# A diffusion layer on one core: a third block normed between value blocks, and the mixer's transfers tied in source order

## The chip, the core and the metric

The kernel runs on one NeuronCore of a Trainium2 chip. The metric is the device time of one execution in microseconds (us). PE is the matrix engine, PEld its weight load, DVE the vector engine, ACT the scalar engine, POOL the GpSimd engine, and SP the engine whose only work here is to issue every DMA of the program, one after the other in the order of its own instruction list.

## What is computed

One layer with fp32 inputs over 17 chunks of 128 tokens: one chunk of context and 16 of latent tokens. The layer norms and modulates its input, projects it, runs a short convolution and a bidirectional gated scan (mLSTM), projects back, and ends with a gated feed-forward network.

```
h = rmsnorm(x, norm1) * (1 + scale1) + shift1
z = h @ w_in                            # sc_b, sc_c, sc_x, q, k, v, o, gates
y_sc = sc_b * conv3(sc_c * sc_x)
h_m = mlstm_bidir(q, k, v, gates)       # per chunk of 128, 4 heads, forward and backward
h_m = rmsnorm(h_m) * mh_norm * sigmoid(o)
x = x + gate1 * (concat(y_sc, h_m) @ w_out)
h2 = rmsnorm(x, norm2) * (1 + scale2) + shift2
up = conv3(h2 @ w_up);  a, gg = split(up)
x = x + gate2 * ((silu(gg) * a) @ w_down);  y = rmsnorm(x, final_norm)
```

## The kernel before

Every large product is made of three: each fp32 operand is split into a rounded high part and a rest (`wh`/`wl` for weights, `hH`/`hL` for activations), and `wh*hH + wh*hL + wl*hH` is added up in a PSUM bank. So a weight tile goes through four steps before PE can use it: a DMA into `wst` (two buffers), a rounding on ACT (`wh`, L111), two subtractions on DVE (`wl`, L114), and then PE. `wh` and `wl` have four buffers each.

The 2176 tokens are six blocks of 384 (the last of 256). Blocks 3 to 5 (`BB`) go first, blocks 0 to 2 (`BA`) second. For `BB`, the value and gate products (`vg`, L378), the k and q heads, the short convolution and the o heads are done in the opening stage, while DVE prepares the modulation beside them. While the o heads of `BB` run, `make_h` norms the blocks of `BA` one by one: `apply` multiplies by the spread inverse norms (DVE, L177), adds the shift on ACT (L181, L185, L186) and takes the rest on DVE (L182, L187), for eight tiles of a block. Then `vg(BA)` follows: per chunk and half one PSUM bank, 24 matmuls, and a small DVE addition (`gates`, L395) that lets go of the bank.

After that come the two woven stages. `weave` walks over units, each a chunk and a pair of heads, 34 in all, and puts blocks of projection work (`fill`) between the units:

- `Sums`: per unit a transposition of k (PE, L792, to PSUM tile `S`), a copy `kT` (ACT, L794), the weighting of v (DVE), two products into `y` (PE, L803), copies of the result (ACT, L814) and a store of the state to `sD`. The fill is the q heads and then the o heads of `BA`: for each head one weight tile, three gemms of 24 matmuls (one for each block), and for each gemm a copy `row` on ACT (L403) and a store to `qD` or `oD` (L404).
- `Mix`: per unit the scores (PE, L850), mask, exponentials and weights (DVE L851, ACT L855, DVE L858 and L859), the output products (PE, L873 and L875), normalization on DVE (L879 to L888), a transposition (PE, L902), the gating by `o` (DVE, L904), and a store to `yD`. It loads k, q, v, the rows `R`, the states `sb` and, in `second`, `o2`. The fill is the short convolution of `BA` (four rounds of three weight tiles and nine gemms, each round ending in stores to `yD`) and then the output projection (`out_proj`, L451): two blocks at a time are loaded back from `yD` (`xt`, two buffers), split on ACT (L461) and DVE (L462), and multiplied by eight weight tiles.

In source order a unit's loads come two units ahead, a head's weights right before its first gemm, and a round's three weights right before its first gemm:

```
            for h in range(H):
                w = load_w(I["w_in"][w0 + h])
                for b in blocks:
                    head(w, b, h, hs, dst, func, scale)
                    yield
```

The source order isn't the program's order. A scheduler takes the traced instructions and orders them engine by engine, under their true dependences; whatever is free of a dependence can be put earlier. SP's list is made in the same way, and an instruction on it that waits for data holds up all the transfers behind it.

Of the kernel before, what the change touches and what calls it, by code (L numbers as in the profile page):

```python
# [2 lines left out]

# [35 lines left out]
BA = (0, 1, 2)  # L39
# [7 lines left out]
def chunks(b):  # L47
    t0, n = BL[b]
    return range(t0 // P, (t0 + n) // P)


def spans(t0, t1):

    return [(a, b, v) for a, b, v in ((t0, min(t1, P), 0), (max(t0, P), t1, 1)) if a < b]
# [3 lines left out]
def hymba_kernel(ctx: ExitStack, tc: tile.TileContext, I, O):  # L58
    nc = tc.nc
# [42 lines left out]
    def run(g, side=None, every=1):  # L102
        for i, _ in enumerate(g):
            if side and i % every == 0:
                next(side, None)

    def load_w(src, n=1024):
        st = wp.tile([P, WN], F32, name="wst", bufs=2)
        Q.dma_start(st[:, :n], src)
        wh = wp.tile([P, WN], F32R, name="wh")  # L110
        S.activation(wh[:, :n], st[:, :n], AF.Copy)  # L111
        wl = wp.tile([P, WN], F32R, name="wl")
        for a in (0, n // 2):
            V.tensor_sub(wl[:, a:a + n // 2], st[:, a:a + n // 2], wh[:, a:a + n // 2].bitcast(F32))  # L114
        return wh, wl
# [18 lines left out]
    def spread(r, n):  # L134

        ps = pst.tile([P, 512], F32, name="st")
        for i in range((n + P - 1) // P):
            w = min(P, n - i * P)
            PE.matmul(ps[:, i * P:i * P + w], bc(r[:w, i:i + 1], [w, P]), ident[:w, :w], start=True, stop=True)
        return ps  # L140

    def load_x(b, src, pool, name, bufs):
        t0, n = BL[b]
        xt = []
        for kh in range(2):
            x = pool.tile([P, 4, 384], F32, name=name, bufs=bufs)
            Q.dma_start(x[:, :, :n], src[4 * kh:4 * kh + 4, :, t0:t0 + n].rearrange("k p t -> p k t"))
            xt.append(x)
        return xt

    def rcol(b):
        t0, n = BL[b]
        return rc[:, t0 // P:(t0 + n) // P]
# [12 lines left out]
        return ss  # L166

    def apply(b, xt, norm):
        t0, n = BL[b]
        rb = spread(rcol(b), n)  # L170
        hH, hL = h_pair()
        sh = 0 if norm == 0 else 24
        for k in range(KT):
            x = xt[k // 4][:, k % 4]
            for a, e, v in spans(t0, t0 + n):
                a, e = a - t0, e - t0
                V.scalar_tensor_tensor(x[:, a:e], x[:, a:e], ab[:, norm, k, v:v + 1], rb[:, a:e],  # L177
                                       op0=ALU.mult, op1=ALU.mult)
                sv = modT[:, sh + k, v:v + 1]
                if k % 2 == 0:  # L180
                    S.activation(hH[:, k, a:e], x[:, a:e], AF.Identity, bias=sv)  # L181
                    V.scalar_tensor_tensor(hL[:, k, a:e], x[:, a:e], sv, hH[:, k, a:e].bitcast(F32),  # L182
                                           op0=ALU.add, op1=ALU.subtract)
                else:
                    S.activation(x[:, a:e], x[:, a:e], AF.Identity, bias=sv)  # L185
                    S.activation(hH[:, k, a:e], x[:, a:e], AF.Copy)  # L186
                    V.tensor_sub(hL[:, k, a:e], x[:, a:e], hH[:, k, a:e].bitcast(F32))  # L187
        return hH, hL

    def h_pair():  # L190
        pool = hps[next(turn) % 3]
        return [pool.tile([P, KT, 384], F32R, name=n) for n in ("hH", "hL")]

    def make_h(b, src, norm):
        return apply(b, load_x(b, src, xp, "xt", 2), norm)

    def accumulator():
        pool = pa[next(turn_a) % len(pa)]
        return pool.tile([P, 512], F32, name="acc")
# [154 lines left out]
    with ExitStack() as ph1:  # L354
        wp = ph1.enter_context(tc.tile_pool(name="wp", bufs=4))
        xp = ph1.enter_context(tc.tile_pool(name="xp", bufs=2))
# [18 lines left out]
        def load_vg(j):  # L375
            return [load_w(I["w_vg"][j, kk], WN) for kk in range(2)]

        def vg(blocks, hs, ws):  # L378
            for b in blocks:
                hH, hL = hs[b]  # L380
                for j in range(2):
                    for c in chunks(b):
                        o = c * P - BL[b][0]
                        acc = accumulator()
                        for k in range(KT):
                            w_h, w_l = (x[:, (k % 4) * 264:(k % 4 + 1) * 264] for x in ws[2 * j + k // 4])
                            a_h, a_l = hH[:, k, o:o + P], hL[:, k, o:o + P]
                            PE.matmul(acc[:, :264], a_h, w_h, start=(k == 0), stop=False)
                            PE.matmul(acc[:, :264], a_h, w_l, start=False, stop=False)
                            PE.matmul(acc[:, :264], a_l, w_h, start=False, stop=(k == KT - 1))  # L390
                        r = rq.tile([P, 2, 129], F32, name="rv", bufs=4)
                        G.memset(r[:, :, 128:129], 1.0)
                        S.activation(r[:, :, :P], acc[:, :256].rearrange("p (h d) -> p h d", h=2), AF.Copy)
                        Q.dma_start(vD[c][:, 2 * j:2 * j + 2], r)
                        V.tensor_add(gates[:, c, j * 8:(j + 1) * 8], acc[:, 256:264],  # L395
                                     bgate[:, j * 8:(j + 1) * 8])
                        yield
# [8 lines left out]
        def heads(blocks, hs, w0, dst, func, scale, by_block=False):  # L406
            if by_block:
                ws = [load_w(I["w_in"][w0 + h]) for h in range(H)]
                for b in blocks:
                    for h in range(H):  # L410
                        head(ws[h], b, h, hs, dst, func, scale)
                        yield
                return
# [5 lines that stand above are left out]
# [89 lines left out]
        hs = {}  # L508
        with tc.tile_pool(name="start", bufs=1, side="right") as stp, \
# [28 lines left out]
            inv_rms(ss, 384, rcol(3))  # L538
            mods(4, 8)
            hs[3] = apply(3, xs[3], 0)  # L540
            ws += load_vg(1)
            Q.dma_start(bgate, I["b_gate"].to_broadcast([P, 16]))
# [24 lines left out]
            def prep(b):  # L567
                xs[b] = load_x(b, I["x"], stp, "xs", 4)
                ss = squares(b, xs[b])
                yield  # L570
                inv_rms(ss, BL[b][1], rcol(b))
                yield
                hs[b] = apply(b, xs[b], 0)
                yield
# [48 lines left out]
            go = heads(BB, hs, 20, oD, AF.Sigmoid, 1.0, by_block=True)  # L623
            for b in BA:
                run(islice(go, 4), side)
                hs[b] = make_h(b, I["x"], 0)
            run(side)
            pa.pop()

# [196 lines left out]
        class Mix:  # L826
# [71 lines left out]
            def third(self):  # L898
# [7 lines left out]
                t0 = (c + 1) * P  # L906
                Q.dma_start(yD[4 + 2 * hp:6 + 2 * hp, :, t0:t0 + P].rearrange("h d t -> d h t"), o2)

        def weave(units, fill, blocks):

            n = len(units)
            for i in range(-1, n + 3):
                if 0 <= i < n:
                    units[i].first()
                if 0 <= i - 3 < n:
                    units[i - 3].third()
                if 0 <= i - 1 < n:
                    units[i - 1].second()
                for x in (0, 1) if i < 0 else (i + 2,):
                    if x < n:  # L920
                        units[x].load()
                for _ in range(blocks[i % 3]):
                    next(fill, None)


        run(vg(BA, hs, load_vg(0) + load_vg(1)))
        with tc.tile_pool(name="gt", bufs=1, side="right") as gt:
            gph = gate_phase()
            kh = heads(BA, hs, 16, kD, AF.Copy, 1.0)
# [11 lines left out]
        for hp in range(2):  # L941
# [6 lines left out]
        fill = chain(heads(BA, hs, 12, qD, AF.Copy, QS), heads(BA, hs, 20, oD, AF.Sigmoid, 1.0),  # L948
                     shortconv(BA, hs), out_proj(((0, 1), (2, 3))))
        weave([Sums(c, hp) for c in range(NL - 1, -2, -1) for hp in range(2)], fill, (1, 0, 1))  # L950
        weave([Mix(c, hp) for c in range(-1, NL) for hp in range(2)], fill, (2, 1, 2))
        phr.close()
        slots = {6: slot(6, "right")}
# [8 lines left out]
        last = out_proj(((4, 5),), late)  # L962
# [10 lines left out]
    with ph2:  # L973
# [219 lines left out]
        for w, (hf, x) in enumerate(PRODS):  # L1193
            n = HN[hf] // 2 // NP[hf]
# [114 lines left out]
```

## Time and profile before

| what | value |
|---|---|
| median of 3 runs | 2507.28 us (2504.99 to 2508.83) |
| profiled execution, its own time | 2504.05 us |
| its span, first to last instruction | 2502.2 us |
| mean granted TensorE clock over the span | 0.992 of full speed |
| PE / PEld / DVE / ACT / POOL busy | 98% / 96% / 69% / 44% / 3% |
| q and o heads with `Sums` (about 500 to 640 us) | PE busy 139.76 of 140 us |
| `Mix` with convolution and output projection (640 to 935 us) | PE busy 285.35 of 295 us |

How to read it: busy times are per engine and overlap. PE's busy share says that it had a matmul in hand, not at which clock; the granted clock stands in the windows view beside it. Times are from the span's start, and L numbers are lines of the kernel before; in the changed kernel the same statements stand some lines further down (L109 and L114 where they were, L404 at L408, L770 at L778, L803 at L811).

### The profile page before, as it was taken

How to read it: one execution, taken by the hardware profiler on the slowest of the kernel's cores; microseconds unless marked ns; L12 is line 12 of the kernel's file. 1: busy time of each engine (PE TensorE's matmuls, PEld its weight loads, DVE VectorE, ACT ScalarE, POOL GpSimd, SP SyncE). 2: the span in 40 equal slices, each digit the busy share in tenths (PEclk: the TensorE clock that was granted, in tenths of full speed). 3: DMA queues.
4: the chain of work that ended last, by engine and by line, in shares of the span. 5: the costliest groups of instructions: out<-in, count | busy, mean ns of one | idle time of the engine just before them, and what ended most of it. 6: DMA issues, size and time to landing. Idle time of an engine off the chain costs nothing.

```text
span 2502.2 us, 44204 instructions
## 1 busy us (share of the span) xinstructions
PE 2454.3 (98%) x17043; PEld 2398.2 (96%) x17043; DVE 1731.5 (69%) x3327; ACT 1100.3 (44%) x2109; POOL 62.9 (3%) x128
## 2 busy tenths in 40 slices
PE   8999999999999989999999999999999999999998
PEld 7999999999999989999999999999999988889998
DVE  4895443433467777789888888776767788677665
ACT  4511133333334444455455445554545454443343
POOL 0000000000011111000000000000000000000000
PEclk9999999999999999999999999999999999999999
DMA  8798723466567886877456446644454476576544
GB/s 276 264 288 257 251 93 112 136 204 205 183 198 213 250 276 198 279 253 259 149 196 217 144 161 212 219 147 168 146 168 147 164 269 233 191 272 207 183 154 151
DMA packets 252437, 506.18 MB, mean 202 GB/s; under 512 B 22962, under 2 KB 153154, under 8 KB 241346
## 3 DMA queue, kind: packets, MB, share of 16 engines
q1 hardware_dynamic: 252226, 503.35, 60.9%
q8 instruction: 134, 2.20, 0.4%
q14 instruction: 77, 0.63, 0.1%
HBM read 355.24 MB, written 148.03 MB: 201 GB/s over the span
## 4 chain that ended last, share of the span: by engine, by line
PE 79%; DMA 8%; DVE 8%; issue 1%; ACT 1%; SPq 1%; POOL 0%; DVEq 0%; ACTq 0%; POOLq 0%
PE pa L1148 7%; PE pa L1150 7%; PE pa L1149 7%; PE acc L206 6%; PE acc L208 6%; PE acc L207 6%; PE pb L1150 4%; PE pb L1148 3%; PE pb L1149 3%; DVE jk L560 3%; PE pa L1206 3%; PE pa L1207 3%; PE pa L1208 3%; DMA wD<-wm 2%; PE pc L1208 2%; PE pc L1206 2%
## 5 line engine op out<-in xcount | busy, mean ns | idle before, releaser
L206 PE MATMUL acc<-hH,wh 128*128 128x384 f32 (+1 forms) x1536 | 514.9, 335 | 5.5 <-DVE cr L430 4.1
L208 PE MATMUL acc<-hH,wl 128*128 128x384 f32 (+1 forms) x1536 | 505.9, 329 | 0.5 <-DVE wl L114 0.5
L207 PE MATMUL acc<-hL,wh 128*128 128x384 f32 (+1 forms) x1536 | 504.9, 329 | 0.0
L1148 PE MATMUL pa<-tH,wh 128*128 128x272 f32 x1408 | 408.5, 290 | 3.8 <-DVE row L488 2.7
L1150 PE MATMUL pa<-tH,wl 128*128 128x272 f32 x1408 | 407.2, 289 | 0.0
L1149 PE MATMUL pa<-tL,wh 128*128 128x272 f32 x1408 | 405.1, 288 | 0.0
L278 ACT ACTIVATE wh<-st 128x512 fp32r<-128x512 f32 (+1 forms) x312 | 189.0, 609 | 403.1 <-PE pa L1149 108.7
L206 PEld LDWEIGHTS acc<-hH,wh 128*128 128x128 f32 x1536 | 291.1, 190 | 8.0 <-DVE cr L430 4.7
L208 PEld LDWEIGHTS acc<-hH,wl 128*128 128x128 f32 x1536 | 290.9, 189 | 1.2 <-DVE wl L114 0.9
L207 PEld LDWEIGHTS acc<-hL,wh 128*128 128x128 f32 x1536 | 291.1, 190 | 0.7
L989 DVE SCALAR_TENSOR_TENSOR tt<-raw,fw,tt 128x127 f32<-128x127 f32 (+4 forms) x264 | 242.3, 947 | 49.3 <-ACT tt L995 48.2
L1148 PEld LDWEIGHTS pa<-tH,wh 128*128 128x128 f32 x1408 | 264.9, 188 | 4.8 <-DVE row L488 2.9
L279 DVE TENSOR_TENSOR wl<-st,wh 128x512 fp32r<-128x512 f32 (+1 forms) x312 | 205.4, 660 | 91.3 <-ACT wh L278 87.9
L1149 PEld LDWEIGHTS pa<-tL,wh 128*128 128x128 f32 x1408 | 265.4, 188 | 0.0
L1150 PEld LDWEIGHTS pa<-tH,wl 128*128 128x128 f32 x1408 | 264.7, 188 | 0.0
L1148 PE MATMUL pb<-tH,wh 128*128 128x272 f32 x704 | 203.6, 289 | 0.4 <-ACT wh L278 0.4
L1150 PE MATMUL pb<-tH,wl 128*128 128x272 f32 x704 | 203.6, 289 | 0.0
L1149 PE MATMUL pb<-tL,wh 128*128 128x272 f32 x704 | 202.7, 288 | 0.0
L278 ACT ACTIVATE wh<-s 128x512 fp32r<-128x512 f32 x176 | 110.9, 630 | 146.5 <-PE pc L1149 90.1
L114 DVE TENSOR_TENSOR wl<-wst,wh 128x512 fp32r<-128x512 f32 (+1 forms) x160 | 105.9, 687 | 64.2 <-ACT wh L111 64.2
L279 DVE TENSOR_TENSOR wl<-s,wh 128x512 fp32r<-128x512 f32 x176 | 120.7, 687 | 29.0 <-ACT wh L278 25.4
L1148 PEld LDWEIGHTS pb<-tH,wh 128*128 128x128 f32 x704 | 132.4, 188 | 0.6 <-ACT wh L278 0.6
(236 smaller groups left out, 5222.0 us busy)
## 6 DMA issues: line engine op xcount, KB each, us to landing
st<-in_w_up SPq DMA_DIRECT2D x88, 512.0 KB, 4.6
wst<-in_w_in SPq DMA_DIRECT2D x48, 512.0 KB, 4.1
wU<-s SPq DMA_DIRECT2D x22, 1024.0 KB, 6.5
s<-wU SPq DMA_DIRECT2D x22, 1024.0 KB, 5.7
st<-wD SPq DMA_DIRECT2D x32, 704.0 KB, 5.2
st<-in_w_down SPq DMA_DIRECT2D x28, 704.0 KB, 4.0
R<-nD SPq DMA_DIRECT2D x34, 512.0 KB, 5.4
wm<-in_w_modr SPq DMA_DIRECT2D x32, 512.0 KB, 3.7
```

The source lines that it names most:

```text
L114: V.tensor_sub(wl[:, a:a + n // 2], st[:, a:a + n // 2], wh[:, a:a + n // 2].bitcast(F32))
L206: PE.matmul(acc[:, :n], w_h, hH[:, k, :n], start=(k == 0), stop=False)
L207: PE.matmul(acc[:, :n], w_h, hL[:, k, :n], start=False, stop=False)
L208: PE.matmul(acc[:, :n], w_l, hH[:, k, :n], start=False, stop=(k == KT - 1))
L278: S.activation(wh[:, :n], a, AF.Copy)
L279: V.tensor_sub(wl[:, :n], a, wh[:, :n].bitcast(F32))
L989: V.scalar_tensor_tensor(o, i, w, o, op0=ALU.mult, op1=ALU.add)
L1148: PE.matmul(acc, wh[:, w], rh, start=(kk == 0 and i in (0, 1, 5)), stop=False, skip_group_check=True)
L1149: PE.matmul(acc, wh[:, w], rl, start=False, stop=False, skip_group_check=True)
L1150: mm = PE.matmul(acc, wl[:, w], rh, start=False, stop=(kk == 3), skip_group_check=True)
L1206: PE.matmul(acc[p], wh[:, k], th[:, t], start=(c == kk == 0), stop=False, skip_group_check=True)
L1208: PE.matmul(acc[p], wl[:, k], th[:, t], start=False, stop=(c == 2 and kk == nk - 1), skip_group_check=True)
```

## The change

Two edits.

1. `apply` becomes a generator, `apply_to`. For block 2 it isn't run while the o heads of `BB` go; it is drained one tile of eight at a time, one after each value product of `vg(BA)`.
2. In `weave`, each piece of source (a unit's `first` and `third`; its `second` with the loads; each fill block) is put under `queued()`: every DMA traced in the piece must stand behind the last DMA traced ahead of the piece. The tie is on the order of SP's list alone, with no semaphore; inside a piece, and on other engines, the scheduler orders as before.

```diff
-from contextlib import ExitStack
+from contextlib import ExitStack, contextmanager
...
     def apply(b, xt, norm):
+        hH, hL = h_pair()
+        run(apply_to(hH, hL, b, xt, norm))
+        return hH, hL
+
+    def apply_to(hH, hL, b, xt, norm):
         t0, n = BL[b]
         rb = spread(rcol(b), n)
-        hH, hL = h_pair()
...
                     S.activation(hH[:, k, a:e], x[:, a:e], AF.Copy)
                     V.tensor_sub(hL[:, k, a:e], x[:, a:e], hH[:, k, a:e].bitcast(F32))
-        return hH, hL
+            yield
...
                 run(islice(go, 4), side)
-                hs[b] = make_h(b, I["x"], 0)
+                if b < 2:
+                    hs[b] = make_h(b, I["x"], 0)
+                else:
+                    hs[b] = h_pair()
+                    third = apply_to(*hs[b], b, load_x(b, I["x"], xp, "xt", 2), 0)
...
+        @contextmanager
+        def queued():
+
+            traced = nc.cur_bb.bb.instructions
+            n = len(traced)
+            last = next(i.name for i in reversed(traced) if i.engine == mybir.EngineType.SP)
+            yield
+            for i in traced[n:]:
+                if i.engine == mybir.EngineType.SP:
+                    tc.add_manual_dep(i, last, mybir.DependencyInfo(
+                        mybir.DependencyClass.NoSync, mybir.DependencyReason.DATA), reason="queued")
+
         def weave(units, fill, blocks):
 
             n = len(units)
             for i in range(-1, n + 3):
-                if 0 <= i < n:
-                    units[i].first()
-                if 0 <= i - 3 < n:
-                    units[i - 3].third()
-                if 0 <= i - 1 < n:
-                    units[i - 1].second()
-                for x in (0, 1) if i < 0 else (i + 2,):
-                    if x < n:
-                        units[x].load()
+                with queued():
+                    if 0 <= i < n:
+                        units[i].first()
+                    if 0 <= i - 3 < n:
+                        units[i - 3].third()
+                with queued():
+                    if 0 <= i - 1 < n:
+                        units[i - 1].second()
+                    for x in (0, 1) if i < 0 else (i + 2,):
+                        if x < n:
+                            units[x].load()
                 for _ in range(blocks[i % 3]):
-                    next(fill, None)
-
-
-        run(vg(BA, hs, load_vg(0) + load_vg(1)))
+                    with queued():
+                        next(fill, None)
+
+
+        run(vg(BA, hs, load_vg(0) + load_vg(1)), third)
+        run(third)
```

What moves, as the built programs list it. The first place is the seam between two heads in `Sums`. On SP, the weights of q head 1 are `wst_5195` (head 2: `wst_5391`, head 3: `wst_5566`), the q row of head 0 and block 2 is `row_5171`, and `row_4...` are rows of the k heads, a stage earlier. Before:

```order
L109 DMA wst_5030<-in_w_in 128x1024
L109 DMA wst_5195<-in_w_in 128x1024
L404 DMA kD_63<-row_4527 128x384
L404 DMA kD_63<-row_4555 128x384
L404 DMA kD_63<-row_4607 128x384
L109 DMA wst_5391<-in_w_in 128x1024
L404 DMA kD_63<-row_4642 128x384
L404 DMA kD_63<-row_4686 128x384
L404 DMA kD_63<-row_4714 128x384
L671 DMA nD_68<-rw_4730 64x128
L109 DMA wst_5566<-in_w_in 128x1024
```

With the change:

```order
L829 DMA sD_67<-sb_5018 128x516
L778 DMA k2_5142<-kD_63 128x2x128
L783 DMA v2_5144<-vD_66 128x258
L408 DMA qD_64<-row_5171 128x384
L778 DMA k2_5191<-kD_63 128x2x128
L829 DMA sD_67<-sb_5115 128x516
L783 DMA v2_5193<-vD_66 128x258
L109 DMA wst_5195<-in_w_in 128x1024
L408 DMA qD_64<-row_5227 128x384
```

The weights of all q heads stood among the stores of the k heads; now those of head 1 stand behind the store of head 0's last row, and behind a state's store and two loads of the piece between.

On PE at the same seam, `acc_5146` is head 0's last gemm and `acc_5202` the first of head 1, which needs `wh_5197`, made of `wst_5195`. Before:

```order
L208 MATMUL acc_5146<-hH_3854,wl_5034 128x384
L792 MATMUL S_5174<-ident_79,k2_5121 128x128 x2
L803 MATMUL y_5181<-vw_5130,kT_5128 128x258
L803 MATMUL y_5182<-vw_5130,kT_5128 128x258
L206 MATMUL acc_5202<-hH_3474,wh_5197 128x384
L207 MATMUL acc_5202<-hL_3475,wh_5197 128x384
L208 MATMUL acc_5202<-hH_3474,wl_5199 128x384
```

With the change:

```order
L800 MATMUL S_5174<-ident_79,k2_5121 128x128 x2
L811 MATMUL y_5181<-vw_5130,kT_5128 128x258
L811 MATMUL y_5182<-vw_5130,kT_5128 128x258
L800 MATMUL S_5230<-ident_79,k2_5142 128x128 x2
L811 MATMUL y_5237<-vw_5179,kT_5177 128x258
L811 MATMUL y_5238<-vw_5179,kT_5177 128x258
L811 MATMUL y_5258<-vw_5235,kT_5233 128x258
L811 MATMUL y_5259<-vw_5235,kT_5233 128x258
L800 MATMUL S_5251<-ident_79,k2_5191 128x128 x2
L811 MATMUL y_5307<-vw_5256,kT_5254 128x258
L811 MATMUL y_5308<-vw_5256,kT_5254 128x258
L210 MATMUL acc_5202<-hH_3470,wh_5197 128x384
```

One transposition and one unit's products stood between the two gemms; now three transpositions and four units' products do, and the three gemms of a head stand close together behind them.

The second place is the start of the output projection's first pair of blocks, on SP. `xt_8762` and `xt_8772` are the two halves of block 0 read back from `yD`, `xt_8785` and `xt_8795` those of block 1, `wst_8806` the first tile of `w_out`, and `yr_8666` the convolution's last row. Before:

```order
L843 DMA sb_8521<-sD_67 128x516
L770 DMA o2_8477<-oD_65 128x2x128
L444 DMA yD_69<-yr_8244 128x384
L459 DMA xt_8762<-yD_69 128x4x384
L770 DMA k2_8630<-kD_63 128x2x128
L770 DMA q2_8634<-qD_64 128x2x128
L907 DMA yD_69<-o2_8124 128x2x128
L839 DMA R_8519<-nD_68 128x1024
L775 DMA v2_8632<-vD_66 128x258
L770 DMA o2_8594<-oD_65 128x2x128
L843 DMA sb_8638<-sD_67 128x516
L459 DMA xt_8772<-yD_69 128x4x384
```

With the change:

```order
L448 DMA yD_69<-yr_8666 128x384
L915 DMA yD_69<-o2_8477 128x2x128
L778 DMA o2_8714<-oD_65 128x2x128
L778 DMA k2_8750<-kD_63 128x2x128
L783 DMA v2_8752<-vD_66 128x258
L778 DMA q2_8754<-qD_64 128x2x128
L847 DMA R_8756<-nD_68 128x1024
L851 DMA sb_8758<-sD_67 128x516
L463 DMA xt_8762<-yD_69 128x4x384
L463 DMA xt_8772<-yD_69 128x4x384
L109 DMA wst_8806<-in_w_out 128x1024
L109 DMA wst_8813<-in_w_out 128x1024
```

The halves of block 0 stood apart, far ahead of the store of `yr_8666`; now they stand behind it, behind the loads of a unit, and next to each other, with the weights after them. The second pair of blocks (`xt_10022` and on) stands in the same way.

The third place is DVE in the value products of `BA`. `gates` are the additions that let go of a bank, `hL_3855` (now `hL_3847`) and `xt_3848` (now `xt_3848` and `xt_3850`) belong to block 2, and `wl` to the value weights. Before:

```order
L177 SCALAR_TENSOR_TENSOR xt_3848<-xt_3848,ab_87,st_3850 128x384 x2
L114 TENSOR_TENSOR wl_3927<-wst_3923,wh_3925 128x528
L187 TENSOR_TENSOR hL_3855<-xt_3848,hH_3854 128x384
L182 SCALAR_TENSOR_TENSOR hL_3855<-xt_3848,modT_86,hH_3854 128x384
L114 TENSOR_TENSOR wl_3934<-wst_3930,wh_3932 128x528
L187 TENSOR_TENSOR hL_3855<-xt_3848,hH_3854 128x384
L114 TENSOR_TENSOR wl_3934<-wst_3930,wh_3932 128x528
L395 TENSOR_TENSOR gates_138<-acc_3937,bgate_135 128x8
L395 TENSOR_TENSOR gates_138<-acc_3967,bgate_135 128x8
L395 TENSOR_TENSOR gates_138<-acc_3997,bgate_135 128x8
```

With the change:

```order
L114 TENSOR_TENSOR wl_3895<-wst_3891,wh_3893 128x528 x2
L399 TENSOR_TENSOR gates_138<-acc_3905,bgate_135 128x8
L181 SCALAR_TENSOR_TENSOR xt_3848<-xt_3848,ab_87,st_3935 128x384 x3
L186 SCALAR_TENSOR_TENSOR hL_3847<-xt_3848,modT_86,hH_3846 128x384
L181 SCALAR_TENSOR_TENSOR xt_3848<-xt_3848,ab_87,st_3935 128x384
L186 SCALAR_TENSOR_TENSOR hL_3847<-xt_3848,modT_86,hH_3846 128x384
L181 SCALAR_TENSOR_TENSOR xt_3850<-xt_3850,ab_87,st_3935 128x384
L114 TENSOR_TENSOR wl_3902<-wst_3898,wh_3900 128x528 x2
L399 TENSOR_TENSOR gates_138<-acc_3942,bgate_135 128x8
L191 TENSOR_TENSOR hL_3847<-xt_3848,hH_3846 128x384 x2
L399 TENSOR_TENSOR gates_138<-acc_3976,bgate_135 128x8
L186 SCALAR_TENSOR_TENSOR hL_3847<-xt_3850,modT_86,hH_3846 128x384
```

The first gate addition stood behind all of block 2's norm and all value weights; now it and the next ones stand between the tiles of that norm.

## The prediction

> **What bounds the kernel now.** I read the stages first, since both edits lie between 380 and 960 us: the windows view by stage, then PE's waits there. Columns of a window: its length, busy time (instructions) of PE, PEld, DVE, ACT, POOL, granted clock, DMA share, GB/s.
>
> ```profile
> 390.00:400.00 10.00, 6.06 (x31) 5.87 (x31) 4.80 (x14) 2.96 (x8) 0.22 (x3) 0.66 0.47 133
> 400.00:410.00 10.00, 10.00 (x85) 10.00 (x84) 0.91 (x6) 1.55 (x4) 0.30 (x3) 1.00 0.12 40
> 500.00:640.00 140.00, 139.76 (x786) 132.86 (x786) 49.61 (x113) 50.88 (x148) 0.00 (x0) 1.00 0.68 206
> 640.00:935.00 295.00, 285.35 (x1839) 283.86 (x1837) 201.52 (x625) 126.60 (x366) 31.18 (x56) 0.99 0.72 223
> 680.00:860.00 180.00, 180.00 (x1184) 180.00 (x1183) 127.12 (x401) 79.08 (x235) 21.02 (x38) 1.00 0.71 217
> 880.00:960.00 80.00, 70.80 (x414) 69.85 (x413) 58.94 (x178) 37.08 (x106) 9.88 (x16) 0.89 0.87 271
> ```
>
> ```profile
> PE S L850 <- DVE R L859: 5.1, 2, 4.6
> PE st L128 <- DVE o L904: 4.4, 1, 4.4
> PE acc L388 <- DVE gates L395: 3.9, 1, 3.9
> ```
>
> PE bounds it, and there is little left to gain. In the heads with `Sums` (500 to 640 us) PE stands still for 0.24 us. There are three real waits (the rows give total, times, longest): one in the value blocks at 391 us, and two near the end of `Mix`, where DVE is late. Each costs more than its length, because the granted clock is low for some time behind it. I count the loss in matmuls. At 390 us 31 were done in 10 us where the next window did 85: 10 x (1 - 31/85) = 6.4 us lost. From 880 to 960 us 414 were done; at the 1184/180 = 6.58 per us of the undisturbed stretch it would be 526, so 112/6.58 = 17.0 us are lost. Together 23.4 us: all that this change can win.
>
> What makes the near end of `Mix` late shows in the other engines' waits there:
>
> ```profile
> DVE R L851 <- DMA R<-nD: 51.0, 22, 5.2
> SPq L770 <- DMA yD<-o: 49.1, 26, 4.2
> ```
>
> SP stands 26 times at a load of `o2` until a store issued just before it has landed, and the rows `R` behind it come late to DVE.
>
> **The third block.** The edit adds and removes no instruction. DVE reaches the `gates` addition of the first value product without the rest of block 2's norm in front, so the bank comes free at once. What is late next is the second pair of value weights:
>
> ```profile
> 381.76 0.37 PE L388 MATMUL acc<-wh,hH 128*128 128x264 f32 x1
> 389.01 1.07 ACT L111 ACTIVATE wh<-wst 128x1056 fp32r<-128x1056 f32 x1
> 393.72 0.70 DVE L114 TENSOR_TENSOR wl<-wst,wh 128x528 fp32r<-128x528 f32 x1
> ```
>
> Their last rounding ended at 390.1 us, and a subtraction behind it takes 0.70. Three products of the first pair (3 x 24 matmuls at 8.5 per us, 8.5 us) keep PE busy from 381.8 to 390.3 us, so a wait of up to half a microsecond is left. The moved steps (eight tiles, each two or three operations on DVE and one or two on ACT of about 0.6 us) now lie beside value products, in the stretch where DVE was busy for 0.91 of 10 us. I take 5 of the 6.4 us; bounds 0 and 6.4.
>
> **The tie: what it removes.** In `Mix`, the `o2` load stands behind the store of the unit just done, whose buffer it doesn't need, so the 4 us stalls of SP go, and `R` is issued two units ahead. This should remove the two late waits as they are: bounds 0 and 17.0, taken 14, because the second pair of output-projection blocks begins there and has a new wait, priced below.
>
> **The tie: what it adds.** Before, a head's weights are loaded a stage early, and the next wait in the chain is for a free buffer, not for a transfer:
>
> ```profile
> ACT wh L111 <- PE acc L207: 29.8, 8, 3.8
> ```
>
> With the tie, SP issues the weights of head h+1 only behind the store of head h's last row, which waits for that gemm. SP's list cannot be overtaken, so from the end of one head's gemms to the start of the next there is a chain, and PE has only the few `Sums` units that stand between. The prices, in the heads stage:
>
> ```profile
> L403 ACT ACTIVATE row<-acc x24: 469/491/492, 501.8 to 634.4; 128x384 f32<-128x384 f32 x24
> 504.24 0.37 SPq L770 DMA_DIRECT2D k<-kD  x1
> 504.99 0.32 SPq L404 DMA_DIRECT2D qD<-row  x1
> DMA to landing us min/median/max: 4.1/4.3/4.5
> L111 ACT ACTIVATE wh<-wst x8: 1057/1057/1058, 510.6 to 633.5; 128x1024 fp32r<-128x1024 f32 x8
> L796 DVE TENSOR_TENSOR vw<-v,cols x30: 686/689/696, 505.7 to 618.1; 128x516 f32<-128x516 f32 x30
> L814 ACT ACTIVATE sb<-y x64: 267/280/291, 505.1 to 624.1; 128x129 f32<-128x129 f32 x64
> 515.90 0.38 PE L792 MATMUL S<-ident,k 128*128 128x128 f32 x2
> 517.00 0.38 PE L792 MATMUL S<-ident,k 128*128 128x128 f32 x2
> ```
>
> (ns min/median/max for the groups; the landing row is of the weight loads, L109.) At least: row 0.49 + four issues (q store, k, state store, v) of 0.32 to 0.37 = 1.33 + landing 4.3 + rounding 1.06 = 7.2 us. Two units back to back take 1.10 us each on PE (515.90 to 517.00), so four units fill about 4.2 us with three transpositions. PE waits 3.0 us. Every second seam has one more unit and three more issues: 8.2 against 5.3, 2.9 us. At most: the state store waits for a unit's products and copies (0.9 + 2 x 0.28), which puts the v load behind it at about 2.3; the last unit in the gap needs that v (about 4.1 to land, as the weights), 0.69 for `vw` and 0.9 for its products, and ACT's list has the rounding behind that unit's first copy, so the gemm starts at about 9.3 and PE waits 5.1; with the extra unit 6.2. There are seven such seams (four q heads, four o heads): between 7 x 3 = 21 and 4 x 5.1 + 3 x 6.2 = 39 us. I take 31, nearer to the upper end since the state store does wait for its unit.
>
> The eighth seam, from the last o head to the convolution, has one context unit in it: two products and copies (about 2), store and issue 0.7, 4.3, 1.06 make 8 us, less 1 us of PE work: 7, in one piece, so with a low clock behind it. By the stretch at 390 us, 6.4 lost for a 3.9 wait, that adds 2.5: 9 us.
>
> In `Mix` there are five seams: three rounds of the convolution and two pairs of output-projection blocks.
>
> ```profile
> 685.97 0.61 PE L850 MATMUL S<-q,k 128*128 128x128 f32 x4
> 688.19 0.39 PE L875 MATMUL y<-v,R 128*128 128x129 f32 x2
> L443 DVE TENSOR_TENSOR yr<-acc,yr 128x384 f32<-128x384 f32 x12 | 6.6, 553 | 3.6 <-PE acc L208 3.4
> L851 DVE TENSOR_TENSOR R<-R,maskN 128x512 f32<-128x512 f32 x27 | 18.6, 690 | 51.0 <-DMA R<-nD 51.0
> L858 DVE TENSOR_TENSOR qs<-R,q 128x512 f32<-128x512 f32 x26 | 17.6, 677 | 0.0
> L859 DVE TENSOR_TENSOR R<-S,R 128x512 f32<-128x512 f32 x30 | 20.5, 682 | 12.4 <-PE S L850 12.4
> L882 DVE TENSOR_SCALAR hv<-y,den 128x128 f32<-128x128 f32 x56 | 19.2, 345 | 0.0
> L883 DVE SCALAR_TENSOR_TENSOR hv<-y,den,hv 128x128 f32<-128x128 f32 x56 | 19.4, 348 | 0.2
> L888 DVE SCALAR_TENSOR_TENSOR sf<-sf,decB,sb 128x129 f32<-128x129 f32 x52 | 17.5, 340 | 0.0
> L904 DVE SCALAR_TENSOR_TENSOR o<-st,mhn,o 128x128 f32<-128x128 f32 x54 | 16.6, 341 | 0.0
> L461 ACT ACTIVATE hH<-xt 128x384 fp32r<-128x384 f32 x32 | 14.4, 510 | 18.3 <-DMA xt<-yD 18.3
> DMA to landing us min/median/max: 5.5/5.5/5.6
> ```
>
> A unit takes PE 2.4 us (from 685.97, its eighth product starting at 688.19) and DVE 0.69 + 0.68 + 0.68 + 2 x (0.345 + 0.348 + 0.340 + 0.341) = 4.8 us. First and third round: 0.55 (L443) + store 0.33 + seven issues 2.45 + 4.3 + 1.06 = 8.7 us against three units, 7.3: at least 1.4; if DVE paces the units, 3 x 4.8 - 7.3 = 7.1. Second round: the weights stand right behind the store, 6.2 against 4.9: 1.3 to 4.7. I take 4.5, 3 and 4.5. A pair of blocks needs both halves of its first block (the last row is the landing of `xt`, 5.5): 3.3 to the first issue, 0.4 to the second, 5.5, four roundings 2.0, and the weights' rounding 1.06 behind them on ACT: 12.3 against three and a half units, 8.5: at least 3.8; the halves of the other block wait for the same two buffers, which can add as much again and more: up to 10. I take 8 for each.
>
> Whether the many shorter waits bring the low clock too is read from a wait of the next stage:
>
> ```profile
> 1080.00:1084.00 4.00, 1.43 (x13) 1.22 (x11) 2.71 (x4) 1.63 (x2) 0.00 (x0) 1.00 1.06 421
> 1084.00:1088.00 4.00, 3.92 (x31) 3.92 (x32) 1.13 (x3) 2.52 (x4) 0.00 (x0) 1.00 0.88 244
> ```
>
> 2.6 us of standing still left the clock at 1.00. The new waits in the seams come in pieces, with transpositions and products between, so I add nothing for the clock but at the eighth. [...]
>
> **The sum.** Added: 31 + 9 + 12 + 16 = 68 us (least 21 + 7 + 4 + 8 = 40, most 39 + 9 + 19 + 20 = 87). Removed: 5 + 14 = 19 (0 to 23). Net +49: the profiled 2504.05 becomes 2553; the median shown is 3.2 us above that execution, so 2556. The ends 40 - 23 and 87 - 0 give 2524 and 2594.
>
> **Rivals.** Faster: the seams are covered and only the 23.4 us go, 2507 - 23 = 2484. That decides where the weights are usable within PE's 4.2 us of units; the landing alone takes 4.3 and the rounding 1.06, which speaks against it. It wins over the forecast below 23.4/13 = 1.8 us per seam. No change: seams at their least and savings at their most still leave 17 us, so it would take savings that I don't see, or a list that SP runs past: about 2507. Much slower: each seam's wait is one piece long enough for the low clock, which adds 12 x 2.5 = 30 us, 2586. For it speaks that some waits are estimated at 5 us or more; against it, the units in between. [...]
>
> **Chances.** Forecast 0.70 (its own range 2524 to 2594), much slower 0.17, faster 0.08, no change 0.05. Within 0.2%, or 5 us, is about what a measurement of this kernel can't tell from no change. Slower 0.87, same 0.05, faster 0.08. The range reaches up to the rival with the clock: 2522 to 2600.
>
> **What would show it.** Right: PE waits for `wh` (L111) or `wl` at seven seams between 480 and 660 us, 3 to 6 us each; ACT waits at L111 for the transfer of `wst` instead of for PE; that stage is 30 to 45 us longer; the waits of L388 for `gates` and of L770 for `yD<-o` are gone. Wrong: the stage from 500 us still full, or the weights issued while the head before is computed.

## The result and the profile after

| what | before | after |
|---|---|---|
| median | 2506.14 us (4 runs) | 2604.21 us (4 runs, 2594.06 to 2613.34) |
| ratio, 95% interval | | 1.0403 [1.037, 1.0436] |
| span of the profiled execution | 2502.2 us | 2600.6 us |
| mean granted TensorE clock | 0.992 | 0.979 |

The change costs 98 us where 49 were forecast. Five marks divide the difference of the two spans, 98.4 us: the last value product, the first score of `Mix`, the last addition of the convolution (on DVE; the others are on PE), the last transposition of `Mix` and the first product of the up projection.

| stretch | before | after | difference | forecast |
|---|---|---|---|---|
| to the last value product | 440.4 | 431.3 | -9.1 | -5 |
| to the first score (q and o heads with `Sums`) | 210.6 | 274.8 | +64.2 | +40 |
| to the end of the convolution | 181.0 | 199.9 | +18.9 | +12 |
| to the last transposition (output projection) | 171.9 | 184.9 | +13.0 | 16 - 14 = +2 |
| to the first up product | 80.2 | 89.1 | +8.9 | 0 |
| the rest | 1418.1 | 1420.6 | +2.5 | 0 |

The windows view by these marks, from the first transposition of `Sums` to the up projection (columns: length, busy time and instructions of PE, PEld, DVE, ACT, POOL, granted clock, DMA share, GB/s) gives the reason for each. First the kernel before:

```profile
499.40:651.00 151.60, 151.37 (x854) 144.44 (x852) 52.72 (x120) 51.80 (x150) 0.00 (x0) 1.00 0.68 209
651.00:832.00 181.00, 181.00 (x1183) 181.00 (x1182) 122.03 (x382) 78.21 (x226) 19.73 (x36) 1.00 0.64 196
832.00:1003.90 171.90, 162.03 (x1004) 160.45 (x1003) 125.18 (x380) 75.15 (x214) 20.18 (x34) 0.95 0.78 243
1003.90:1084.10 80.20, 77.55 (x520) 77.29 (x518) 64.36 (x141) 38.87 (x79) 1.95 (x2) 1.00 0.89 290
```

And after:

```profile
486.20:706.10 219.90, 180.72 (x878) 160.54 (x877) 58.91 (x123) 59.41 (x150) 0.00 (x0) 0.90 0.46 138
706.10:906.00 199.90, 188.33 (x1156) 185.13 (x1155) 116.87 (x367) 70.70 (x215) 18.86 (x36) 0.96 0.55 167
906.00:1090.90 184.90, 168.76 (x1031) 164.77 (x1030) 133.18 (x395) 83.22 (x231) 18.72 (x34) 0.94 0.80 256
1090.90:1180.00 89.10, 81.40 (x519) 80.26 (x517) 66.59 (x145) 41.07 (x81) 1.96 (x2) 0.96 0.90 288
```

Length minus PE's busy time is idle time; length times (1 - clock) is what the low clock takes. Idle: 0.2 + 0 + 9.9 + 2.7 = 12.8 us before, 39.2 + 11.6 + 16.1 + 7.7 = 74.6 after, so 61.8 more. Clock: 0 + 0 + 8.6 + 0 before, 22.0 + 8.0 + 11.1 + 3.6 = 44.7 after, so 36.1 more. The two make 97.9 of the 109.1 us by which the four rows are longer: waiting, and the slow clock behind the waits. Of the other 11.2 us some 4 are 23 products more that stand in the rows (3584 against 3561), and 1.5 come from the rounding of the clock's column (added up from rows of 1 us, the clock takes 46.1 us after and 8.5 before). About 6 us stay open.

What PE waits for between 340 and 1220 us (total, times, longest), then in the heads stage alone (486 to 706 us), and what SP, ACT and DVE wait for from 480 to 690 us:

```profile
PE acc L210 <- ACT wh L111: 22.7, 14, 6.7
PE y L811 <- DVE vw L804: 22.4, 12, 3.3
PE y L881 <- DVE qs L866: 6.6, 3, 3.0
PE st L231 <- ACT rb L233: 6.2, 3, 4.1
```

```profile
PE y L811 <- DVE vw L804: 22.4, 12, 3.3
PE acc L210 <- ACT wh L111: 12.7, 9, 6.7
```

```profile
SPq L408 <- ACT row L407: 107.8, 17, 13.9
ACT wh L111 <- DMA wst<-in_w_in: 10.0, 3, 5.2
DVE vw L804 <- DMA v<-vD: 95.4, 25, 11.1
```

SP stands 107.8 of 210 us at the row stores, for a row that ACT copies at the end of a gemm. The weights and v stand behind these stores on SP's list, and PE waits for both: at the seven seams between heads mostly for v (22.4 us, and 5.9 for weights), at the eighth for weights alone (6.7).

One seam, between two q heads, row by row (start, length, engine, line, operation, and in brackets the idle time and its releaser):

```profile
503.06 0.34 PE L212 MATMUL acc<-hH,wl 128*128 128x384 f32 x1
503.46 1.04 PE L811 MATMUL y<-vw,kT 128*128 128x258 f32 x4
503.95 0.32 SPq L408 DMA_DIRECT2D qD<-row  x1
505.34 0.42 SPq L783 DMA_DIRECT2D v<-vD  x1
505.81 0.44 SPq L109 DMA_DIRECT2D wst<-in_w_in  x1
507.12 0.44 PE L800 MATMUL S<-ident,k 128*128 128x128 f32 x2 [0.25 <-DMA k<-kD]
510.04 0.70 DVE L804 TENSOR_TENSOR vw<-v,cols 128x516 f32<-128x516 f32 x1 [2.46 <-DMA v<-vD]
510.88 1.94 PE L811 MATMUL y<-vw,kT 128*128 128x258 f32 x4 [3.32 <-DVE vw L804]
512.17 1.05 ACT L111 ACTIVATE wh<-wst 128x1024 fp32r<-128x1024 f32 x1
513.27 0.69 PE L210 MATMUL acc<-hH,wh 128*128 128x384 f32 x1 [0.45 <-ACT wh L111]
```

From the end of the last product of one head (503.40) to the first of the next it is 9.9 us (the prediction's ends: 7.2 and 9.3). The weights leave SP 1.86 us behind the row's store, and the last unit's v just ahead of them. The long idle piece, 3.32 us, is the wait for that v. The four products behind it take 1.94 us instead of the 1.04 of the units before: the granted clock is 0.50 there (read in single us, from 511 to 514.4 us).

### The profile page after: what moved, and what is told of

It is laid out like the page before. It is cut to its first block, busy times and chain, and to the rows that moved or that the text cites. A ratio compares the mean times of both kernels' runs of the same rounds, so it can differ in the third digit from the quotient of the medians.

```text
span 2600.6 us, 44070 instructions
## 1 busy us (share of the span) xinstructions
PE 2495.6 (96%) x17043; PEld 2418.7 (93%) x17043; DVE 1738.3 (67%) x3327; ACT 1106.4 (43%) x2109; POOL 60.6 (2%) x128
## 4 chain that ended last, share of the span: by engine, by line
PE 71%; DMA 13%; DVE 9%; ACT 3%; SPq 2%; issue 2%; POOL 0%; DVEq 0%; ACTq 0%
PE pa L1172 7%; PE pa L1174 7%; PE pa L1173 7%; PE acc L210 5%; PE acc L211 5%; PE acc L212 5%; PE pb L1174 3%; PE pb L1172 3%; PE pb L1173 3%; DVE jk L564 3%; PE pa L1232 2%; PE pa L1231 2%; PE pa L1230 2%; PE pc L1173 2%; PE pc L1174 2%
## 5 line engine op out<-in xcount | busy, mean ns | idle before, releaser
L210 PE MATMUL acc<-hH,wh 128*128 128x384 f32 (+1 forms) x1536 | 520.3, 339 | 27.4 <-ACT wh L111 22.7
L211 PE MATMUL acc<-hL,wh 128*128 128x384 f32 (+1 forms) x1536 | 513.7, 334 | 0.0
L210 PEld LDWEIGHTS acc<-hH,wh 128*128 128x128 f32 x1536 | 298.8, 195 | 35.1 <-ACT wh L111 29.1
L211 PEld LDWEIGHTS acc<-hL,wh 128*128 128x128 f32 x1536 | 297.9, 194 | 0.2 <-issue 0.2
```

What stands on the lines that cost most here:

```text
L210: PE.matmul(acc[:, :n], w_h, hH[:, k, :n], start=(k == 0), stop=False)
L211: PE.matmul(acc[:, :n], w_h, hL[:, k, :n], start=False, stop=False)
```

## Experiments

All ratios are to the kernel before, which was timed anew beside each group of runs (medians of 2500.25, 2503.49 and 2501.94 us).

### The two edits and the two stages apart

The third block alone (`weave` as before, without `queued`):

```
-                with queued():
                 ...
         run(vg(BA, hs, load_vg(0) + load_vg(1)), third)
```

> Edit 1 alone: block 2 is normed between the value products, no transfer is tied. If its gain is real and separate: the last value matmul ends 6 to 9 us earlier than before (440.4 us) and the whole is 6 to 9 us faster, about 2498 us, with PE full from 380 to 440 us. Rival: the gain is given back in the next stage, 2506 us.

The tie in `Sums` alone, the third block normed as before, then the tie in `Mix` alone (False and True exchanged):

```
-        weave([Mix(c, hp) for c in range(-1, NL) ...], fill, (2, 1, 2))
+        weave([Mix(c, hp) for c in range(-1, NL) ...], fill, (2, 1, 2), tied=False)
```

> The tie alone and in the scan stage (Sums) alone, without edit 1. If the stages add up: the stage from the first transposition to the first score is about 60 us longer and the rest as before, about 2567 us. Rival, that the lost time of the scan stage is made up or caused elsewhere: under 2540 us or over 2590 us.

> The tie alone and in the output stage (Mix) alone, without edit 1. If the stages add up: 98 + 8 - 60 us above before, about 2552 us, of it some 20 us in the convolution's rounds, 13 in the output projection and 9 behind it. Rival: the tie of the output stage gains by itself (the stalls at the store of o2 are gone) and what was lost there came from the scan stage's late end: under 2510 us.

Measured: third block 0.9984 [0.9974, 0.9994], 2495.87 against 2500.25 us, so 4.4 us where 6 to 9 were expected; tie in `Sums` 1.0242 [1.0224, 1.0261]; tie in `Mix` 1.0165 [1.0145, 1.0185]. In us -4.4 + 58.8 + 40.6 = 95, so the parts add up to the whole within the intervals. In the kernel with the tie in `Mix` alone the heads stage is as full as before, and the later stretches lose nearly what the whole change loses there (heads, convolution, behind `Mix`):

```profile
501.00:653.10 152.10, 151.10 (x854) 144.44 (x853) 49.68 (x114) 54.81 (x148) 0.00 (x0) 1.00 0.56 176
653.10:849.80 196.70, 185.99 (x1158) 182.86 (x1157) 117.10 (x367) 71.72 (x216) 19.29 (x36) 0.97 0.54 170
1033.10:1121.40 88.30, 81.08 (x519) 79.93 (x516) 66.47 (x145) 41.45 (x81) 1.96 (x2) 0.96 0.89 291
```

So the 8.9 us behind `Mix` come with the tie in `Mix` as well, though nothing is tied there; with the tie in `Sums` alone that stretch is 80.7 us, as before.

### Which loads: the weights left out of the tie

```
+    free = set()
...
-        Q.dma_start(st[:, :n], src)
+        free.add(Q.dma_start(st[:, :n], src).ins.name)
...
-                if i.engine == mybir.EngineType.SP:
+                if i.engine == mybir.EngineType.SP and i.name not in free:
```

> Both edits, but the weight loads (wst) are left out of the tie, so that the scheduler may put them ahead again; all other transfers stay tied. Theory that the late weights make the waits: PE full again in the heads stage, the clock at 1.00 there, 2500 to 2530 us. Rival, that the loads of k and v, held behind the stores, make them: PE still stands still some 25 us or more in the heads stage, 2560 us or more.

Measured: 1.0003 [0.9991, 1.0016]. With the weights free nearly all of the loss is gone; the median is 4.6 us above that of the third block alone. k, v, the states, q, o and R were still tied. The heads stage is full again:

```profile
490.10:641.40 151.30, 151.27 (x854) 144.43 (x853) 52.33 (x116) 52.20 (x146) 0.00 (x0) 1.00 0.63 193
821.00:994.80 173.80, 161.97 (x1014) 159.36 (x1015) 133.14 (x393) 81.61 (x230) 22.39 (x34) 0.97 0.86 273
```

What is left, in the second row, are 11.8 idle us in the output projection, in place of the 9.9 of the kernel before.

### k and v left out instead

```
+            if name == "k2":
+                free.add(d.ins.name)
-            Q.dma_start(v2, vD[c][:, 2 * hp:2 * hp + 2])
+            free.add(Q.dma_start(v2, vD[c][:, 2 * hp:2 * hp + 2]).ins.name)
```

> The whole change with only the loads of k and v of the sums left out of the tie; the weights stay in it. Theory (late weights): the products of the sums no longer wait for v, but the next head's first product still waits for its weights, so that the wait changes its name on TensorE (from the products of k and v to those of the head) and the time stays at 1.030 to 1.040. Rival (k and v behind the stores are the cause): the stretch of the sums falls back by more than half of its 59 us, ratio 1.020 or below.

Measured: 1.0243 [1.0219, 1.0267], between both expectations. The wait changed its name as the theory said, to that for weights alone; from 480 to 690 us PE waits

```profile
PE acc L212 <- ACT wh L113: 14.3, 8, 7.1
```

and no longer for `vw`. But it became shorter too:

```profile
489.80:677.50 187.70, 166.75 (x854) 150.80 (x853) 55.41 (x120) 57.26 (x148) 0.00 (x0) 0.95 0.49 159
```

21 idle us instead of 39, and 9 us of low clock instead of 22. The late weights make each seam; the late v, which PE's order places ahead of the next head, lengthens it by about as much again. Neither theory was complete. In the run before, with the weights free, v is still tied and DVE waits 34.5 us for it in the heads stage (longest 4.2; 88.0 us and 11.1 from 490 to 700 us of the change), but PE stands still for none of it. Here, without the late v, the weights cost about half.

### The tie complete, the weights asked for earlier in the source

```
                 for b in blocks:
+                    if b == blocks[1]:
+                        if h + 1 < H:
+                            ahead_w.append(load_w(I["w_in"][w0 + h + 1]))
                         ...
                     head(w, b, h, hs, dst, func, scale)
                     ...
+                    pre = early and b == blocks[-1] and m < 3
+                    if pre:
+                        nxt.append(load_w(I["w_in"][4 + m + 1]))
                     ...
```

The lines with `pre` stand in the convolution's loop, which asks for two of the next round's three weights that way.

> The whole change with the tie complete, but each head's weights asked for earlier in the source: the next head's during this head's second block, and the next convolution round's during this round's last block, so that in source order the load stands several rows' stores ahead of the place where it is needed. Theory (weights late because they stand behind the row store of the head's last block): most of the 59 us that the tie adds in the sums and of the 19 us in the convolution goes; left are the output projection's 13 to 20 us; ratio 1.006 to 1.014. Rival (it is the pacing of the queue as a whole, k and v behind the same stores): the waits move from the weights to v and the time stays above 1.025.

Measured: 1.0121 [1.0097, 1.0145]. The heads stage is whole again with every transfer still in source order, those of k and v too:

```profile
492.50:644.50 152.00, 151.19 (x854) 144.30 (x853) 55.55 (x120) 54.75 (x148) 0.00 (x0) 1.00 0.64 195
644.50:836.10 191.60, 182.22 (x1153) 181.16 (x1152) 116.46 (x367) 70.80 (x215) 17.42 (x36) 0.97 0.57 176
```

In the heads it is not the tie that costs, but the place that the source gives to a load. In the convolution (second row) only 8.3 of the 18.9 us came back, less than expected; the third weight of a round and the pace of the units were not separated there. The output projection's weights keep their place in this kernel, and that stretch and the one behind it stay as long as in the change (183.4 and 87.2 us).

### The clock: work put into the wait

Ten extra products (17.5 us for all seven units) behind the transpositions of k, their result overwritten by the real product; loads and tie as in the change.

```
+                if self.i in (5, 10, 14, 19, 23, 28, 32):
+                    for _ in range(10):
+                        PE.matmul(pk[0][:, :P], self.kT[:, :P], ident, start=True, stop=True)
```

> The whole change as it is, with ten extra products of 128 columns (about 0.26 us each, 2.6 us together, their result is overwritten) put on TensorE right behind the k transposes of seven units of the sums, where the products then wait for v or the head's first products for their weights. If it is the idle time in one piece that lowers the granted clock, the clock at these seams stays near 1.00 though no load comes earlier: the extra products run inside the wait, the heads' stretch from 486 to 680 us gets shorter by 10 to 20 us, and the time falls to a ratio of about 1.033 to 1.036 of before (the whole change: 1.040). Rival: the clock falls there for another reason (few products in a stretch, or the small shapes of the scan), the extra work then lies beside the wait and changes nothing, or adds its 18 us: ratio 1.040 to 1.047.

Measured: 1.0366 [1.0329, 1.0403]; the interval meets that of the whole change, so the time alone would not decide. The seams do. The eight seams of the heads after the change, 13 us each:

```profile
503.00:516.00 13.00, 8.80 (x38) 6.52 (x36) 5.67 (x13) 4.49 (x13) 0.00 (x0) 0.87 0.37 112
529.00:542.00 13.00, 9.00 (x30) 6.49 (x29) 5.96 (x14) 4.24 (x13) 0.00 (x0) 0.74 0.45 138
554.00:567.00 13.00, 8.80 (x34) 6.94 (x33) 5.86 (x13) 4.45 (x13) 0.00 (x0) 0.82 0.43 122
581.00:594.00 13.00, 8.95 (x29) 6.11 (x28) 5.68 (x14) 5.24 (x13) 0.00 (x0) 0.74 0.41 129
605.00:618.00 13.00, 8.62 (x36) 6.27 (x35) 5.99 (x13) 4.70 (x13) 0.00 (x0) 0.87 0.49 141
631.00:644.00 13.00, 8.64 (x29) 6.34 (x28) 5.99 (x14) 4.19 (x12) 0.00 (x0) 0.74 0.47 138
655.00:668.00 13.00, 9.12 (x37) 7.09 (x36) 3.92 (x7) 4.91 (x13) 0.00 (x0) 0.87 0.49 146
680.00:693.00 13.00, 6.28 (x23) 5.93 (x23) 2.77 (x5) 3.67 (x5) 0.00 (x0) 0.74 0.64 197
```

The seven that got extra work:

```profile
505.00:518.00 13.00, 11.63 (x68) 10.06 (x67) 4.74 (x12) 3.88 (x11) 0.00 (x0) 1.00 0.31 98
527.00:540.00 13.00, 9.68 (x42) 8.03 (x41) 5.14 (x12) 3.69 (x10) 0.00 (x0) 0.74 0.43 132
553.00:566.00 13.00, 11.32 (x67) 9.77 (x66) 5.03 (x12) 4.42 (x13) 0.00 (x0) 1.00 0.37 106
577.00:590.00 13.00, 9.72 (x50) 8.35 (x49) 4.88 (x12) 4.73 (x10) 0.00 (x0) 0.87 0.42 126
600.00:613.00 13.00, 11.41 (x67) 9.65 (x66) 5.83 (x13) 4.49 (x13) 0.00 (x0) 1.00 0.46 132
625.00:638.00 13.00, 9.43 (x50) 8.23 (x49) 4.88 (x12) 3.38 (x9) 0.00 (x0) 0.87 0.40 125
650.00:663.00 13.00, 11.36 (x65) 9.41 (x64) 3.21 (x6) 4.32 (x13) 0.00 (x0) 1.00 0.33 97
```

At four seams the extra products fell into the wait for v: 1.4 to 1.7 us of idle time are left, and the clock is 1.00. At the other three the unit whose v is late (a wait of 2.4 to 2.8 us) comes ahead of the extra products on PE, so they don't fill that wait; 3.3 to 3.6 us are left, and the clock falls, to 0.74 and 0.87. Over the seven, the low clock takes 13 x 0.52 = 6.8 us instead of 13 x 1.35 = 17.6. The whole stage:

```profile
487.20:697.40 210.20, 185.63 (x1019) 169.81 (x1017) 57.91 (x122) 59.51 (x150) 0.00 (x0) 0.95 0.47 143
```

It is 9.7 us shorter with 17.5 us more work in it, and idle time and extra work together (24.6 + 17.5 = 42.1) are no less than the 39.2 idle us of the change, so the gain is not that of loads that came earlier. The low clock is the idle time's doing, and it is 10 us here at least.

### Is there a version that gains?

The loads `xt` and `row` of the output projection taken out of the tie as well as the weights; then the same without the third block; then this and the third block alone once more, side by side:

```
+                        free.add(Q.dma_start(yt[:, :, :n], yD[...]).ins.name)
+                        free.add(Q.dma_start(xr[:, :n], I["x"][m][...]).ins.name)
```

> Both edits, with the loads of the weights left out of the tie as in the run before, and the two loads of the output projection (its y columns and its x rows) left out as well; k, v, q, o, R and all the stores stay tied. If every us that the tie adds comes from loads that the filling products need and that stand behind stores which wait for data, the waits that were left at the starts of the two output-projection pairs (at 820 to 834 and 920 to 938 us, some 8 to 10 us together) go, those of the kernel before at 892 and 930 stay away as well, and the time falls to about 2490 us, ratio 0.994 to 0.997 of before, below the third block alone (0.998). Rival: the fill then runs ahead again as it did before and meets the same waits for the scores, so that the time is that of the third block alone, 0.998. A second rival: the y columns were never what the pair starts waited for, and the ratio stays at 1.000.

> The tie alone, over k, v, q, o, R and the stores, with the filling products' loads (weights, y columns, x rows) left out of it, and the third block normed where it was before. Theory: what is left of the tie costs nothing and takes the waits of the kernel before at 892 and 930 us (17.0 us with the low clock, of which new short waits for R and for the last o come back): a ratio of 0.997 to 0.999. Rival: the gain of the same tie with the third block (0.997) was the third block's alone, and the ratio is 1.000 within 0.001.

> The same kernel as the one with the filling products' loads left out of the tie, on the same chip as the tie without the third block and the third block alone: 0.996 to 0.998, the lowest of the three if both edits bring something.

> The third block alone once more, for the same comparison: 0.998 within 0.001. If it is as low as the kernel with both edits, the rest of the tie brings nothing.

| kernel | ratio |
|---|---|
| tie without the fill's loads, and third block | 0.9971 [0.9957, 0.9984], again 0.9970 [0.9958, 0.9982] |
| the same tie without the third block | 0.9990 [0.9978, 1.0002] |
| third block alone | 0.9984 [0.9974, 0.9994], again 0.9968 [0.9956, 0.9980] |

The third block alone is 4.4 and 7.4 us below the kernel before, by the medians. What is left of the tie then adds nothing that these runs can tell. Where only it was put in, PE waits in `Mix` for `R` 6.9 us in four pieces, against 5.1 in two before, and for `o` 2.5 us against 4.4: most of its promised gain is not there.

## Why the prediction was wrong, step by step

The sign was right, and so was the path, weights and v behind the store of a row; the size was half. Taken apart into idle time and clock, the sum of the idle time came out as forecast at nearly every step, though often under another name, and **the step that failed is "I add nothing for the clock but at the eighth"**: the term of 2.5 us for the low clock measured 44.7 us over the four stretches, against 8.6 before, so 36 us more.

- **Third block: right in size.** Forecast 5 us, at most 6.4. From 340 to 440 us (before, then after) PE now does 39 products more, at 7.45 per us 5.2 us; timed, the edit alone gave 4.4 and 7.4. PE no longer waits for `gates`. The mark at the last value product moved by more, 9.1 us, but it varies by some us between kernels that are nearly alike up to there: 428.4 to 433.5 us in the nine with this edit, 436.1 to 441.9 in the four without.

```profile
340.00:440.00 100.00, 96.06 (x706) 95.87 (x705) 38.04 (x99) 38.18 (x83) 1.43 (x14) 0.97 0.35 109
340.00:440.00 100.00, 100.00 (x745) 99.96 (x744) 41.39 (x108) 43.48 (x91) 1.43 (x14) 1.00 0.34 109
```

- **Seven head seams: idle right, clock missed.** Forecast 31 us of waits; the first seven rows above have 91 - 61.9 = 29.1. The path was the one given as the upper end, through the last unit's v. But the sign that was named for it, PE waiting 3 to 6 us for `wh` or `wl` at each seam, did not come: for `wh` it waits 0.5 to 1.0 us, for `vw` 2.6 to 3.7. The clock took 17.6 us more in these rows, for which nothing was set. With the eighth seam the stage grew by 68 us, where 30 to 45 were named as a sign.
- **Eighth seam: right.** It is the one where PE waits for `wh` alone. Forecast 7 + 2.5; the row at 680 us has 6.7 idle and 0.26 x 13 = 3.4 of clock.
- **Convolution: idle right, clock missed.** Forecast 12, idle 11.6, clock 8.0. Only 4.0 of the 11.6 are waits for the weights; the larger part are waits for DVE's steps of the units (`qs`, `hv`, `sf`, `den`), the case that the prediction set as its upper end.
- **Output projection: idle right, saving as forecast, clock missed.** The two late waits went (for `o` 0.7 us are left, for `R` 1.4; SP no longer waits for the store `yD<-o` ahead of the `o2` load), and the pairs cost 7.85 and 8.20 idle us, forecast 8 each. But the clock, whose loss was counted among the savings, is low at the new waits for 0.26 x 20 + 0.25 x 22 = 10.7 us:

```profile
908.00:928.00 20.00, 12.15 (x66) 10.41 (x65) 16.57 (x57) 11.06 (x32) 1.87 (x4) 0.74 0.82 276
1012.00:1034.00 22.00, 13.80 (x69) 11.93 (x70) 17.04 (x57) 12.93 (x37) 4.35 (x7) 0.75 0.89 288
```

- **Behind `Mix`: not in the sum.** 5 us more of idle time and 3.6 of clock, at `st L231 <- rb`. The runs tie it to the weights in `Mix` (80.8 us there with the weights free, 80.2 before, 87 to 89 in every kernel with the output projection's weights in the tie). In the longest of these waits (4.1 us, ended at 1137.94) `rb` stands on ACT's list right behind the steps on `F` (L245), which wait for DVE, which had waited 3.5 us for the load of `F`. How late weights bring that about stays open.

Why the clock step failed: from one wait of 2.6 us that left the clock at 1.00 the prediction took a safe length, and it counted on the units to break up the waits. The units did not: their products stood behind the v that was late too, so the longest idle piece of a seam was 1.4 to 3.3 us, with shorter pieces around it. Nor was the length safe (last section). The rival "much slower", given 0.17, had this mechanism, with 2.5 us at each of 12 seams; it fell 18 us short as well, for 5.2 us at a pair and the stretch behind `Mix`.

## What to carry to other kernels

When an issuing engine's list is put into source order, look at every load that stands behind a store of computed data: it is issued when that data is done, however early its buffer is free, and what it feeds must be covered for issue, landing and rounding (here 9.9 us at the seam shown, where the prediction counted on 4.2 us of products). Leave such a load out of the order, which removed nearly all of the cost here, or ask for it one step earlier in the source, which removed that of the heads. In the sum, give the clock behind new waits on the matrix engine a term of its own: in this kernel 62 us of idle time brought 36 of clock, and none (the clock stayed at 1.00) at the four seams where extra work stood inside the wait.

## What the runs showed of the hardware

The clock was lost in whole portions, and shorter waits cost it than the trace of before suggested. After the change, the slow stretches between 340 and 1240 us run at 0.50 for 3.4 us (eight of them), 6.8 us (eight) or 10.2 us (one); before, two of 6.8 us and one of 10.2. At the seam shown, the clock is 0.50 from 511.0 to 514.4 us and then 1.00, a loss of 1.7 us; a stretch of 6.8 us takes twice that: the seams' rows show 0.87 (13 x 0.13 = 1.7) and 0.74 (3.4). The row with 0.82 ends inside a slow stretch, which lasts until 569 us and takes 3.4 as well. In the three short ones of these eight stretches PE is idle for 0 to 0.5 us, in the five long ones for 0.8 to 1.7.

And the length of the wait doesn't decide alone. In the kernel with k and v left out of the tie, one wait of 1.67 us ahead of 509.88 us did it, with 0.41 us of idle time two us ahead of it:

```profile
508.00:509.00 1.00, 0.21 (x1) 0.00 (x0) 0.08 (x1) 0.23 (x1) 0.00 (x0) 1.00 1.10 345
509.00:510.00 1.00, 0.12 (x1) 0.12 (x2) 0.14 (x1) 1.00 (x3) 0.00 (x0) 1.00 1.06 313
510.00:511.00 1.00, 1.00 (x4) 1.00 (x5) 1.00 (x2) 0.27 (x2) 0.00 (x0) 0.57 0.66 187
511.00:512.00 1.00, 1.00 (x5) 1.00 (x4) 0.15 (x1) 0.00 (x0) 0.00 (x0) 0.50 0.59 153
```

The 2.6 us at 1081 us of the kernel before didn't: the clock is 1.00 in both of the prediction's rows there. At the seventh seam after the change the longest piece was 1.43 us, with one of 0.98 behind it, and the clock fell to 0.50 from 664.6 to 668.0 us. So waits shorter than the one that the prediction took as safe did lower it. What decides is not shown.
